# When the expert rows of three token groups are gathered in a one-layer decoder step: all of the first two ahead of the one-hot gates, those of the last tile from its first pair of heads

## The chip, the cores and the metric

The kernel runs on one core of a Trainium2 chip (trn2). The metric is device time in microseconds (us) of one execution, from the runtime's own count; lower is better. The engines are named as in the profile: PE (TensorE matmul, with PEld its weight load), DVE (VectorE), ACT (ScalarE), POOL (GpSimd), SP (SyncE, which only issues DMAs here).

## The reference, cut to what matters

One layer of a decoder serves 512 prompt tokens (four tiles of 128) and 32 sample tokens. After the token mixing every token goes through an expert retrieval: for each of 8 heads it scores 128 + 128 sub-keys, takes the 16 best of each half, the 16 best of their sums, and so has 128 experts per token, each a row of `expert_u` and a row of `expert_v` (16384 x 1024 each, f32).

```
s1, i1 = lax.top_k(s[:, :, 0], PEER_TOPK)
s2, i2 = lax.top_k(s[:, :, 1], PEER_TOPK)
...
idx = jnp.take_along_axis(cidx, sel, axis=-1).reshape(PEER_BLOCK, PEER_HEADS * PEER_TOPK)
gate = jax.nn.softmax(top, axis=-1).reshape(PEER_BLOCK, PEER_HEADS * PEER_TOPK)
pre = jnp.einsum('td,tkd->tk', hb, eu[idx]).astype(F32)
act = jax.nn.gelu(pre, approximate=False) * gate
return jnp.einsum('tk,tkd->td', act.astype(hb.dtype), ev[idx])
```

## The kernel before, in words

The retrieval is done in two ways.

**Gathered**, for prompt tiles 0 and 3 and for the samples (`experts`, lines 1067 to 1100). For each k, POOL issues an indirect DMA (line 1075) that brings one row of `expert_u` per partition, 128 rows of 4 KB, into one of six buffers (tile `gat`); DVE multiplies it with the normed input and sums it (a *dot*: `CUSTOM_DVE_ANT_0` and the read of its sum into `pre`). When all dots are done, ACT applies Gelu, and the rows of `expert_v` come the same way; DVE adds each, scaled, to an accumulator `x` (an *add*: `SCALAR_TENSOR_TENSOR`). A prompt tile has 128 dots and 128 adds, the samples (packed four heads' groups to the partitions) have 32 and 32, and after them four small sums (tile `h`, 32x1024) and a norm, `finish` (line 1101). A row is used two gathers after it was issued (`LAG`), and the buffers are `GAT` = 6. Each gather is one step of a Python generator; `side` is the list of generators, and `beside(n)` takes n steps from the first of them.

**Dense**, for tiles 1 and 2. `gates` (line 1423) makes a 128 x 128 matrix of gates per token out of one-hot matmuls: for 8 tokens a step, DVE compares (tiles `uH`, `uL`, and two of eight columns in `vH`), ACT scales six columns, PE multiplies, ACT copies the result away. Sixteen steps make tile 1's gates, sixteen tile 2's. The gates also carry, by `next(more)`, the late part of tile 3: output projection, norm and query projection (`late`, line 1553). Then a loop over 128 blocks of experts (line 1644) does all 16384 experts for the 256 tokens: per block PE transposes and multiplies, DVE makes the low parts `uL`, `aL` and applies the gates (`w`), ACT casts, POOL makes `vL` (line 1498).

**What sets the order.** All engines work their queues in order. The queues are written at compile time by a scheduler that takes instructions in the order of the code (of *tracing*) as long as its own timeline says they can start; `tc.issue_after(m)` adds that what is traced inside stands behind instruction `m` on its engine. Before, the rows of tile 0 and of the samples are 320 gathers: 280 steps (`AHEAD`) are traced by a loop ahead of the gates, each only bound to stand behind the DVE instruction that was last when tile 0's rows were put on the list; during the 32 gate steps 0.8 steps each (`RATE_G`), behind the last DVE instruction of that gate step; the rest in the dense loop, 1.6 steps a block (`RATE_H`) as long as tile 3 is being decoded and 2.4 (`RATE_D`) after that.

The decode of tile 3 (`late_heads`, line 1607) runs one step a block in the dense loop. Its 8 heads come as four pairs. Two pairs share the second half of `head_steps` (line 995): the first pair only finds its top 16, then the second pair does so and the index work is done for all four heads. After two pairs (64 of 128 columns of `ei` known) tile 3's rows are put on the list.

```
1619    for n in range(AHEAD):
1620        with tc.issue_after(marks[gather_mark[0]]):
1621            beside(1)
1622    more = late()
...
1652        next(more, None)
1653        with tc.issue_after(mark), tc.issue_after(sub):
1654            beside(RATE_H if coming[0] else RATE_D)
```

Of the kernel before, what the change touches and what calls it, by code (L numbers as in the profile page):

```python
# [32 lines left out]
LAG = 2  # L33
WST = 3
UV = 5
AHEAD = 280
RATE_G = 0.8
RATE_D = 2.4
RATE_H = 1.6
LATE = 2  # L40
# [69 lines left out]
def bc(ap, shape):  # L110
    return ap.to_broadcast(shape)
# [3 lines left out]
def hymba_step(ctx, tc, x_prompt, x_sample, cache_k, cache_v, state_wkv, state_shift, meta, norm1_g, w_in, mu, w0,  # L115
# [4 lines left out]
    marks = []  # L120
# [124 lines left out]
    side, due = [], [0.0]  # L245

    def beside(n):

        due[0] += n
        while side and due[0] >= 1.0:  # L250
            due[0] -= 1.0
            if next(side[0], None) is None:
                side.pop(0)
        due[0] = min(due[0], 1.0)
# [875 lines left out]
    def tile_experts(i, ei, ga, h2, x2=None):  # L1130
        def mk():
            if x2 is None:
                box.append(px2())
                G.dma_start(box[0], xscr[i])
            return box[0]
        box = [] if x2 is None else [x2]
        yield from experts(h2, ei, ga, 128, mk, False)
        finish(box[0], gat(), 128, y_p[0, 128 * i:128 * i + 128, :], final_g(gat()))
# [15 lines left out]
    def place(c):  # L1154
        return _t(p0, "ei" + c, 1, [128, 128], I32), _t(p0, "ga" + c, 1, [128, 128])

    plS, pl0, pl1 = place("s"), place("0"), place("1")
# [46 lines left out]
    with ExitStack() as px:  # L1204
# [43 lines left out]
        def put(src, dst):  # L1248

            A.copy(dst[0], src)  # L1250
            V.tensor_tensor(dst[1], src, dst[0].bitcast(F32), OP.subtract)
# [171 lines left out]
    def gates(its, sel, ps, put):  # L1423


        i1T, i2T, gaT = sel
        its, iot = its
        ib = dt_("aH", 2, [128, 2, 128], BF16)
        for c, x in enumerate((i1T, i2T)):
            A.copy(ib[:, c], x)  # L1430
        for n, t8 in enumerate(range(0, 128, 8)):
            ob = dt_("uL", 2, [128, 128, GA], BF16)
            o0, o1 = dt_("uH", 2, [128, 8, 128]), dt_("vH", 2, [128, 8, 128])
            V.tensor_tensor(o0.rearrange("p t j -> p j t"), its, bc(ib[:, 0, t8:t8 + 8].unsqueeze(1), [128, 128, 8]), OP.is_equal)
            V.tensor_tensor(ob, its[:, :, 0:GA], bc(ib[:, 1, t8:t8 + GA].unsqueeze(1), [128, 128, GA]), OP.is_equal)
            for q0 in (0, 4):
                p = ps()
                for q in range(q0, q0 + 4):
                    t = slice(t8 + q, t8 + q + 1)
                    if q < GA:  # L1440
                        A.mul(o1[:, q, :], ob[:, :, q], gaT[:, t])
                    else:
                        V.tensor_scalar(o1[:, q, :], iot, i2T[:, t], gaT[:, t], OP.is_equal, OP.mult)
                    T.matmul(p[:, 128 * (q - q0):128 * (q - q0) + 128], o0[:, q, :], o1[:, q, :], start=True, stop=True)  # L1444
                put(t8 + q0, p)
            if n % LATE:
                next(more, None)
            with tc.issue_after(marks[-1]):
                beside(RATE_G)


    ND = 256
# [3 lines left out]
    def dt_(tag, bufs, shape, dt=F32):  # L1456
        return _t(dn, tag, bufs, shape, dt)
# [148 lines left out]

    def late_heads():

        half = None
        for g in range(4):  # L1610
            if g == 2:
                side.append(tile_experts(3, *pl1, held[0]))
            sc = dt_("lsc", 1, [128, 4, 128])
            DM.dma_start(sc, lscr[g])
            half = yield from head_steps(sc, [x[:, 32 * (g & 2):32 * (g & 2) + 64] for x in pl1], late_tile, half if g % 2 else [])
            yield True
        coming[0] = False

    for n in range(AHEAD):
        with tc.issue_after(marks[gather_mark[0]]):  # L1620
            beside(1)
    more = late()
    its = one_hot_table()
    sels = [sel_transposed(0, dps, dt_("selT", 1, [128, 3, 128])), sel_transposed(1, dps, dt_("lsc", 1, [128, 3, 128]))]
    gates(its, sels[0], dps, stage)
    gates(its, sels[1], dps, keep)
    for _ in more:
        pass
    more = late_heads()
    gl = {}  # L1630

# [68 lines left out]
```

## Time and profile before

| | us |
|---|---|
| three runs | 2180.15, 2190.67, 2161.02; median 2180.15 |
| the profiled execution | 2171.7 |
| its span in the trace | 2169.9 |
| PE, DVE, ACT, POOL busy | 1816.4, 1639.2, 862.6, 1271.9 |

The span is first to last instruction; what lies around it is 1.8 us. The shares of busy time are means over stages that have different limits: the projection and mixing (0 to about 1085 us), the gates (about 1116 to 1247), the dense loop (about 1247 to 2131) and a tail. A line of the grouped views reads: line, engine, operation, written tile <- read tiles, shapes, count | busy time in us, mean ns of one | idle time of the engine just before them and what ended it. All DVE instructions have one line (127, a helper), so they go by tiles.

### The profile page before, as it was taken

To read this page: it belongs to the slowest core of one execution; us is meant where nothing else is said; L and a number is where in the kernel's file an instruction comes from. 1 tells how busy PE (TensorE), PEld (TensorE's weight loads), DVE (VectorE), ACT (ScalarE), POOL (GpSimd) and SP (SyncE) were. 2 spreads that over 40 slices of the span, in tenths; PEclk is the share of its full clock that TensorE was granted. 3 is DMA by queue.
4 is the path that set the end of the run, shared out by engine and by line. 5 is a ranking of instruction groups with operands and counts; after the bars stand their busy time and mean duration, and the time that the engine had idled before them with its cause. 6 is when DMAs were issued, how large, how long until landed. Compare 5 with 4: busy or idle time off the path is not lost.

```text
span 2169.9 us, 37101 instructions
## 1 busy us (share of the span) xinstructions
PE 1816.4 (84%) x13915; PEld 1693.1 (78%) x13915; DVE 1639.2 (76%) x3285; ACT 862.6 (40%) x1975; POOL 1271.9 (59%) x951
## 2 busy tenths in 40 slices
PE   5999984585685868898567998999999999999992
PEld 5888973373574757798457988899999999999992
DVE  5643426679878988678989999867676767899988
ACT  6553421221132322433258943444444444444442
POOL 0110103678777677533824365768776777888885
PEclk9999986555675768799769999999999999999996
DMA  7532373487779789966859985789999998999987
GB/s 222 164 107 81 106 199 108 156 304 237 262 247 308 242 282 323 299 222 206 271 182 330 341 287 191 287 297 392 336 336 336 330 338 330 326 322 328 328 312 261
DMA packets 311306, 571.60 MB, mean 263 GB/s; under 512 B 32916, under 2 KB 194694, under 8 KB 310983
## 3 DMA queue, kind: packets, MB, share of 16 engines
q0 software_dynamic: 84048, 305.70, 39.6%
q1 hardware_dynamic: 227078, 263.53, 37.5%
q8 instruction: 110, 1.80, 0.3%
q14 instruction: 70, 0.57, 0.1%
HBM read 544.12 MB, written 25.65 MB: 263 GB/s over the span
## 4 chain that ended last, share of the span: by engine, by line
PE 56%; DVE 17%; issue 9%; DMA 8%; POOL 7%; ACT 3%; SPq 0%; POOLq 0%; DVEq 0%; ACTq 0%
PE acc L1523 5%; PE acc L1524 5%; PE acc L1522 5%; PE w L1508 5%; PE w L1505 5%; PE w L1506 5%; PE w L1491 4%; POOL gat L1075 4%; PE pD L220 3%; DVE x L127 3%; PE pD L966 2%; DVE gat L127 2%; DMA wst<-in_w_query_dram 2%; PE ps L220 2%; PE w L1444 2%
## 5 line engine op out<-in xcount | busy, mean ns | idle before, releaser
L127 DVE SCALAR_TENSOR_TENSOR x<-gat,act,x 128x1024 f32<-128x1024 f32 x287 | 440.5, 1535 | 12.5 <-DMA gat<-in_expert_v_dram,ei 9.4
L1075 POOL DMA_INDIRECT gat<-in_expert_u_dram,ei x256 | 337.0, 1316 | 132.2 <-DVE pre L127 45.8
L1075 POOL DMA_INDIRECT gat<-in_expert_v_dram,ei x256 | 317.7, 1241 | 122.6 <-issue 35.4
L1498 POOL TENSOR_TENSOR vL<-uv,vH 128x1024 fp32r<-128x1024 f32 x128 | 335.2, 2619 | 84.0 <-ACT vH L1497 82.7
L1522 PE MATMUL acc<-aH,vH 128*128 128x256 f32 x1024 | 292.2, 294 | 6.2 <-ACT aH L1514 6.2
L1523 PE MATMUL acc<-aL,vH 128*128 128x256 f32 x1024 | 289.5, 285 | 7.0 <-DVE aL L127 6.8
L1524 PE MATMUL acc<-aH,vL 128*128 128x256 f32 x1024 | 288.6, 284 | 0.0
L1505 PE MATMUL w<-dhH,uH 128*128 128x256 f32 x1024 | 251.6, 283 | 2.7 <-DVE uL L127 1.5
L1506 PE MATMUL w<-dhL,uH 128*128 128x256 f32 x1024 | 251.3, 283 | 0.0
L127 DVE CUSTOM_DVE_ANT_0 gat<-gat,h 128x1024 f32<-128x1024 f32 x160 | 202.7, 1279 | 44.7 <-DMA gat<-in_expert_u_dram,ei 41.7
L1523 PEld LDWEIGHTS acc<-aL,vH 128*128 128x128 f32 x1024 | 197.2, 193 | 8.9 <-DVE aL L127 8.8
L1505 PEld LDWEIGHTS w<-dhH,uH 128*128 128x128 f32 x1024 | 196.7, 192 | 3.1 <-DVE uL L127 1.7
L1522 PEld LDWEIGHTS acc<-aH,vH 128*128 128x128 f32 x1024 | 192.7, 192 | 7.1 <-ACT aH L1514 7.1
L1524 PEld LDWEIGHTS acc<-aH,vL 128*128 128x128 f32 x1024 | 197.1, 192 | 0.0
L1506 PEld LDWEIGHTS w<-dhL,uH 128*128 128x128 f32 x1024 | 196.7, 192 | 0.0
L1497 ACT CAST vH<-uv 128x1024 fp32r<-128x1024 f32 x128 | 134.9, 1054 | 148.9 <-issue 111.3
L127 DVE TENSOR_TENSOR uL<-w,uH 128x512 fp32r<-128x512 f32 x256 | 166.7, 682 | 10.1 <-ACT uH L1493 10.1
L127 DVE TENSOR_TENSOR w<-w,gl 128x128 f32<-128x128 f32 x128 | 50.3, 393 | 148.6 <-ACT w L1509 148.6
L127 DVE CUSTOM_DVE_ANT_0 gat<-gat,lx 128x1024 f32<-128x1024 f32 x128 | 158.1, 1268 | 0.0
L1508 PE MATMUL w<-dhH,uL 128*128 128x256 f32 x1024 | 148.1, 286 | 4.7 <-DVE uL L127 4.3
L1493 ACT CAST uH<-w 128x512 fp32r<-128x512 f32 x256 | 138.0, 593 | 8.0
L1508 PEld LDWEIGHTS w<-dhH,uL 128*128 128x128 f32 x1024 | 133.0, 192 | 7.6 <-DVE uL L127 6.9
(568 smaller groups left out, 4046.5 us busy)
## 6 DMA issues: line engine op xcount, KB each, us to landing
uv<-in_expert_u_dram SPq DMA_DIRECT2D x128, 512.0 KB, 4.5
uv<-in_expert_v_dram SPq DMA_DIRECT2D x128, 512.0 KB, 6.0
wst<-in_w_query_dram SPq DMA_DIRECT2D x48, 512.0 KB, 6.6
wst<-in_w_out_dram SPq DMA_DIRECT2D x24, 512.0 KB
wst<-in_w_in_dram SPq DMA_DIRECT2D x20, 512.0 KB, 4.4
h2T<-in_w_in_dram SPq DMA_DIRECT2D x20, 512.0 KB, 4.2
gscr<-uv SPq DMA_DIRECT2D x10, 1024.0 KB, 5.9
uv<-in_w_query_dram SPq DMA_DIRECT2D x8, 1024.0 KB, 12.2
```

Of the source, the lines that this page charges most:

```text
L127: r = getattr(nc.vector, name)(*args, **kw)
L220: T.matmul(p[:, 0:n], w[:, k, :], x, start=(k == 0 and x is H and w is wH), stop=(k == 7 and w is wL))
L1075: G.indirect_dma_start(out=r, out_offset=None, in_=w[0], in_offset=bass.IndirectOffsetOnAxis(ap=ei[:, k:k + 1], axis=0))
L1493: A.copy(uH[:, ks, :], p)
L1497: A.copy(vH, vn)
L1498: G.tensor_tensor(vL, vn, vH.bitcast(F32), OP.subtract)
L1505: T.matmul(pre, uH[:, k, :], hH[:, k, :], start=(k == 0), stop=False)
L1506: T.matmul(pre, uH[:, k, :], hL[:, k, :], start=False, stop=False)
L1508: T.matmul(pre, uL[:, k, :], hH[:, k, :], start=False, stop=(k == 7))
L1522: T.matmul(o, vH[:, ds_], aH, start=(j == 0 and d % 2 == 0), stop=False, skip_group_check=True)
L1523: T.matmul(o, vH[:, ds_], aL, start=False, stop=False, skip_group_check=True)
L1524: T.matmul(o, vL[:, ds_], aH, start=False, stop=(j == 127), skip_group_check=True)
```

## The change

1. All steps of the rows of tile 0 and of the samples are traced ahead of the gates (`while side`), and `gates` takes none any more.
2. Tile 3 is decoded pair by pair: each pair runs the whole of `head_steps` by itself, for 2 heads, and its rows are put on the list after the first pair instead of the second.

```
-AHEAD = 280
-RATE_G = 0.8
...
             if n % LATE:
                 next(more, None)
-            with tc.issue_after(marks[-1]):
-                beside(RATE_G)
...
     def late_heads():
 
-        half = None
         for g in range(4):
-            if g == 2:
+            if g == 1:
                 side.append(tile_experts(3, *pl1, held[0]))
             sc = dt_("lsc", 1, [128, 4, 128])
             DM.dma_start(sc, lscr[g])
-            half = yield from head_steps(sc, [x[:, 32 * (g & 2):32 * (g & 2) + 64] for x in pl1], late_tile, half if g % 2 else [])
+            yield from head_steps(sc, [x[:, 32 * g:32 * g + 32] for x in pl1], late_tile)
             yield True
         coming[0] = False
 
-    for n in range(AHEAD):
+    while side:
         with tc.issue_after(marks[gather_mark[0]]):
             beside(1)
```

The rates in the dense loop (1.6 and 2.4) stay. PE's queue is the same up to the first transposes of the dense loop. Three places of the queues follow.

DVE just ahead of the gates: `dsel` is the decode of tile 2 that ends there, `dhL` a low part for the dense loop, `uH` and `vH` the first gate step. Before:

```order
L127 TENSOR_REDUCE dsel_16_111<-ce_7163 128x32
L127 TENSOR_TENSOR ce_7167<-iota_87,hl_7152 128x512
L127 TENSOR_REDUCE dsel_17_112<-ce_7167 128x32
L127 TENSOR_TENSOR ce_7171<-iota_87,hl_7152 128x512
L127 TENSOR_REDUCE dsel_17_112<-ce_7171 128x32
L127 TENSOR_TENSOR dhL<-w_7873,dhH 128x4x128
L127 TENSOR_TENSOR dhL<-w_7880,dhH 128x4x128
L127 TENSOR_TENSOR dhL<-w_7889,dhH 128x4x128
L127 TENSOR_TENSOR dhL<-w_7896,dhH 128x4x128
L127 TENSOR_SCALAR vH_8792<-aL_8771,selT_8775 128x128 x2
L127 TENSOR_TENSOR uH_8791<-vL_8773,aH_8787 128x128x8
```

The same place now; `x_1953` is the samples' accumulator:

```order
L125 TENSOR_REDUCE dsel_17_112<-ce_7171 128x32
L125 SCALAR_TENSOR_TENSOR x_1953_8803<-gat_8847,act_8800,x_1953_8803 128x1024
L125 SCALAR_TENSOR_TENSOR x_1953_8803<-gat_8850,act_8800,x_1953_8803 128x1024
L125 SCALAR_TENSOR_TENSOR x_1953_8803<-gat_8853,act_8800,x_1953_8803 128x1024
L125 SCALAR_TENSOR_TENSOR x_1953_8803<-gat_8856,act_8800,x_1953_8803 128x1024
L125 TENSOR_TENSOR dhL<-w_7873,dhH 128x4x128
L125 SCALAR_TENSOR_TENSOR x_1953_8803<-gat_8859,act_8800,x_1953_8803 128x1024
L125 TENSOR_TENSOR dhL<-w_7880,dhH 128x4x128
L125 SCALAR_TENSOR_TENSOR x_1953_8803<-gat_8862,act_8800,x_1953_8803 128x1024
L125 TENSOR_TENSOR dhL<-w_7889,dhH 128x4x128
L125 TENSOR_TENSOR dhL<-w_7896,dhH 128x4x128
L125 TENSOR_SCALAR vH_8950<-aL_8929,selT_8933 128x128
```

Counted over the whole queue, 11 dots and 22 adds have moved to a place ahead of the first `uH`. The sixteen steps of tile 1's gates had 11 dots and 1 add between them and now have 10 adds, the four small sums and the samples' last scaling; those of tile 2's gates had 12 adds and now none.

DVE in the dense loop's second and third block: `lvals`, `lidx`, `lsc` and `lcand` belong to the decode of tile 3, `x_2051` is the samples' accumulator. Before:

```order
L127 TENSOR_TENSOR uL_10286<-w_10287,uH_10285 128x512
L127 TENSOR_TENSOR uL_10286<-w_10294,uH_10285 128x512
L127 SCALAR_TENSOR_TENSOR x_2051_9243<-gat_10244,act_9240,x_2051_9243 128x1024
L127 MAX lvals_10608<-lsc_10606 128x8 x2
L127 TENSOR_TENSOR aL_10279<-w_10250,aH_10278 128x256
L127 MAX lvals_10608<-lsc_10606 128x8 x2
L127 MAX_INDEX lidx_10230<-lvals_10608,lsc_10606 128x8 x4
L127 MATCH_REPLACE lsc_10606<-lvals_10608,lsc_10606 128x128 x4
L127 MAX lvals_10608<-lsc_10606 128x8 x4
```

Now; `lsm` and `leq` are the index work that before came only after the second pair, `ei` the finished row numbers:

```order
L125 TENSOR_TENSOR uL_10264<-w_10265,uH_10263 128x512
L125 TENSOR_TENSOR uL_10264<-w_10272,uH_10263 128x512
L125 TENSOR_TENSOR aL_10257<-w_10228,aH_10256 128x256
L125 TENSOR_REDUCE lsm_10683<-leq_10767 128x32
L125 MAX lvals_10944<-lsc_10939 128x8 x4
L125 SCALAR_TENSOR_TENSOR ei_11_106<-lsm_10682,lsm_10683 128x32
L125 MAX_INDEX lidx_10941<-lvals_10944,lsc_10939 128x8 x4
L125 MATCH_REPLACE lsc_10939<-lvals_10944,lsc_10939 128x128 x4
L125 MAX lvals_10944<-lsc_10939 128x8 x3
```

Between the last gate step and the 18th `aL`, 19 adds, the four small sums and the scaling are gone, 15 dots of tile 3 stand there instead of 5, and the decode has some 25 instructions more. The row numbers were finished after `aL` 9 and 17 (two pairs each) and are finished after `aL` 2, 5, 9 and 12.

DVE at the end: `uv` is the dense tiles' output, `x_3149` and `x_3145` tile 3's accumulator. Before, with three more adds, a reciprocal and the last scaling behind these rows:

```order
L127 SCALAR_TENSOR_TENSOR uv_21365<-uv_21365,sE_21381,uv_21335 128x1024
L127 SCALAR_TENSOR_TENSOR x_3149_16489<-gat_20635,act_16486,x_3149_16489 128x1024
L127 SCALAR_TENSOR_TENSOR x_3149_16489<-gat_20638,act_16486,x_3149_16489 128x1024
L127 SCALAR_TENSOR_TENSOR x_3149_16489<-gat_20722,act_16486,x_3149_16489 128x1024
L127 SCALAR_TENSOR_TENSOR x_3149_16489<-gat_20725,act_16486,x_3149_16489 128x1024
L127 SCALAR_TENSOR_TENSOR x_3149_16489<-gat_20728,act_16486,x_3149_16489 128x1024
L127 SCALAR_TENSOR_TENSOR x_3149_16489<-gat_20810,act_16486,x_3149_16489 128x1024
L127 SCALAR_TENSOR_TENSOR x_3149_16489<-gat_20813,act_16486,x_3149_16489 128x1024
L127 SCALAR_TENSOR_TENSOR x_3149_16489<-gat_20895,act_16486,x_3149_16489 128x1024
L127 SCALAR_TENSOR_TENSOR x_3149_16489<-gat_20898,act_16486,x_3149_16489 128x1024
L127 SCALAR_TENSOR_TENSOR x_3149_16489<-gat_20901,act_16486,x_3149_16489 128x1024
L127 SCALAR_TENSOR_TENSOR x_3149_16489<-gat_20983,act_16486,x_3149_16489 128x1024
```

Now, to the end of the work:

```order
L125 SCALAR_TENSOR_TENSOR uv_21427<-uv_21427,sE_21443,uv_21397 128x1024
L125 SCALAR_TENSOR_TENSOR x_3145_16314<-gat_20721,act_16311,x_3145_16314 128x1024
L125 SCALAR_TENSOR_TENSOR x_3145_16314<-gat_20724,act_16311,x_3145_16314 128x1024
L125 SCALAR_TENSOR_TENSOR x_3145_16314<-gat_20808,act_16311,x_3145_16314 128x1024
L125 SCALAR_TENSOR_TENSOR x_3145_16314<-gat_20811,act_16311,x_3145_16314 128x1024
L125 SCALAR_TENSOR_TENSOR x_3145_16314<-gat_20814,act_16311,x_3145_16314 128x1024
L125 SCALAR_TENSOR_TENSOR x_3145_16314<-gat_20896,act_16311,x_3145_16314 128x1024
L125 RECIPROCAL sF_20906<-sF_20906 128x1
L125 SCALAR_TENSOR_TENSOR gat_20901<-x_3145_16314,sF_20906,gat_20902 128x1024
```

Behind the last `aL` there were 22 adds and are 14. On POOL, behind the last `vL`, there were 21 gathers and are 12.

## Rows read from the trace of the kernel before

**Rows 1.** Busy time by stage; times are us from the span's start.
```profile
core 0: us, PE busy (x) PEld busy (x) DVE busy (x) ACT busy (x) POOL busy (x), PEclk, DMA share, GB/s
1021.00:1085.00 64.00, 35.04 (x254) 31.85 (x252) 60.29 (x184) 15.73 (x46) 54.33 (x52) 0.83 0.87 276
1085.00:1115.70 30.70, 15.82 (x62) 11.92 (x62) 25.40 (x121) 9.71 (x26) 9.69 (x15) 0.50 0.66 211
1115.70:1172.00 56.30, 39.61 (x256) 36.51 (x256) 53.29 (x83) 47.07 (x121) 20.63 (x10) 0.89 0.79 261
1172.00:1247.00 75.00, 74.32 (x616) 72.05 (x617) 67.29 (x88) 69.80 (x241) 28.18 (x16) 0.97 0.96 332
1247.00:1397.00 150.00, 132.77 (x1048) 127.68 (x1048) 141.96 (x365) 64.88 (x124) 93.38 (x74) 0.97 0.71 249
1397.00:2125.00 728.00, 723.84 (x6104) 722.54 (x6103) 568.44 (x897) 303.64 (x544) 567.39 (x340) 1.00 0.91 330
2125.00:2161.40 36.40, 5.96 (x38) 5.43 (x37) 33.26 (x32) 8.64 (x22) 21.91 (x19) 0.59 0.90 328
```
**Rows 2.** The chain that ended last, from 2100 us on: start, us, what.
```profile
2103.60 0.96 PE w L1508 x8
...
2110.22 0.48 PE w L1508 x4
...
2153.61 6.36 DMA gat<-in_expert_v_dram,ei
2160.06 1.29 DVE x L127
```
**Rows 3.** Issues of SP's queue in order of time, 2080 to 2171.
```profile
2138.64 2.73 SPq L1103 DMA_DIRECT2D out_dram<-uv  x2
2165.61 0.33 SPq L1103 DMA_DIRECT2D out_dram<-gat  x1
```
**Rows 4.** DVE groups, 1085 to 1115.7: line, op, shapes, count | busy, mean ns | idle before.
```profile
L127 DVE TENSOR_REDUCE dsel<-ce 128x32 f32<-128x512 f32 x5 | 3.4, 684 | 4.6 <-POOL ce L1053 4.6
```
**Rows 5.** DVE groups, 1021 to 1087.
```profile
L127 DVE CUSTOM_DVE_ANT_0 gat<-gat,h 128x1024 f32<-128x1024 f32 x21 | 31.7, 1515 | 2.7 <-DMA gat<-in_expert_u_dram,eis 2.7
```
**Rows 6.** DVE groups, 780 to 950.
```profile
L127 DVE SCALAR_TENSOR_TENSOR x<-gat,act,x 128x1024 f32<-128x1024 f32 x71 | 97.1, 1367 | 5.9 <-DMA gat<-in_expert_v_dram,ei 5.4
```
**Rows 7.** DVE groups, 1115.7 to 1172.
```profile
L127 DVE TENSOR_TENSOR uH<-vL,aH 128x1024 f32<-128x1024 bf16 x14 | 26.9, 1934 | 0.0
L127 DVE CUSTOM_DVE_ANT_0 gat<-gat,h 128x1024 f32<-128x1024 f32 x10 | 12.1, 1214 | 0.0
...
L127 DVE DVE_READ_ACCUMULATOR2_ANT pre<- 128x1 f32 x10 | 0.8, 78 | 0.0
```
**Rows 8.** DVE groups, 1172 to 1247.
```profile
L127 DVE SCALAR_TENSOR_TENSOR x<-gat,act,x 128x1024 f32<-128x1024 f32 x13 | 16.7, 1281 | 0.0
```
**Rows 9.** DVE groups, 1247 to 1397.
```profile
L127 DVE SCALAR_TENSOR_TENSOR x<-gat,act,x 128x1024 f32<-128x1024 f32 x18 | 35.3, 1964 | 0.0
...
L127 DVE CUSTOM_DVE_ANT_0 gat<-gat,lx 128x1024 f32<-128x1024 f32 x6 | 10.6, 1786 | 0.0
...
L127 DVE TENSOR_TENSOR h<-h,gat 32x1024 f32<-32x1024 f32 x3 | 4.8, 1584 | 0.4 <-DMA gat<-x 0.4
...
L127 DVE SCALAR_TENSOR_TENSOR gat<-h,sF,gat 32x1024 f32<-32x1024 f32 x1 | 1.3, 1262 | 0.0
...
L127 DVE TENSOR_TENSOR ga<-ga,sR 128x64 f32<-128x64 f32 x2 | 0.4, 211 | 0.0
```
**Rows 10.** DVE groups, 2125 to 2161.4.
```profile
L127 DVE SCALAR_TENSOR_TENSOR x<-gat,act,x 128x1024 f32<-128x1024 f32 x23 | 29.5, 1283 | 2.5 <-DMA gat<-in_expert_v_dram,ei 2.1
```
**Rows 11.** POOL groups, 1021 to 1087.
```profile
L1075 POOL DMA_INDIRECT gat<-in_expert_u_dram,eis x26 | 33.4, 1284 | 10.9 <-issue 3.4 <-DVE pre L127 1.9 <-DVE hl L127 1.8
```
**Rows 12.** POOL groups, 1115.7 to 1247.
```profile
L1075 POOL DMA_INDIRECT gat<-in_expert_v_dram,eis x20 | 38.0, 1900 | 61.0 <-DVE x L127 44.9 <-DVE pre L127 15.8 <-DVE uL L127 0.3
```
**Rows 13.** POOL groups, 1247 to 1397.
```profile
L1498 POOL TENSOR_TENSOR vL<-uv,vH 128x1024 fp32r<-128x1024 f32 x19 | 46.8, 2464 | 18.2 <-ACT vH L1497 18.1
```

More of the change, by code (lines that the diff above doesn't have):

```diff
@@ L35 @@
 UV = 5
-AHEAD = 280
-RATE_G = 0.8
 RATE_D = 2.4
@@ L1447, in gates @@
                 next(more, None)
-            with tc.issue_after(marks[-1]):
-                beside(RATE_G)
     ND = 256
@@ L1607, in late_heads @@
     def late_heads():
-        half = None
         for g in range(4):
-            if g == 2:
+            if g == 1:
                 side.append(tile_experts(3, *pl1, held[0]))
@@ L1614, in late_heads @@
             DM.dma_start(sc, lscr[g])
-            half = yield from head_steps(sc, [x[:, 32 * (g & 2):32 * (g & 2) + 64] for x in pl1], late_tile, half if g % 2 else [])
+            yield from head_steps(sc, [x[:, 32 * g:32 * g + 32] for x in pl1], late_tile)
             yield True
         coming[0] = False
-    for n in range(AHEAD):
+    while side:
         with tc.issue_after(marks[gather_mark[0]]):
```

## The prediction

> **What bounds the kernel now.** I read the table by stage first, because the shares over the whole span mix stages with different limits [rows 1]. The reader should go down its rows and ask which engine fills each stretch. From 1085 to 1115.7 (stage A, end of the decode ahead of the gates) it is DVE: 25.4 of 30.7 us, and the 5.3 us that it idles are mostly waits for POOL's `ce`, 4.6 us in front of one group [rows 4]. From 1115.7 to 1172 (B1, gates of tile 1) it is DVE again, 53.3 of 56.3. From 1172 to 1247 (B2, gates of tile 2 with the query projection) it is PE: 74.3 of 75.0; DVE has 7.7 us to spare. From 1247 to 1397 (C, first blocks of the dense loop) DVE is busy for 142 of 150 and PE for 132.8; so PE waits 17.2 us there. From 1397 to 2125 (D) PE has 723.8 of 728: the chain steps from one L1508 to the next in 2110.22 - 2103.60 = 6.62 us [rows 2], and 728 us are 110 blocks of 6.62. After 2125 PE is done but for a little, and the chain goes through the last gathers and adds of tile 3 [rows 2] while DVE has 33.3 of 36.4 us and the DMA engines 0.90 at 328 GB/s [rows 1]. The dense tiles' output is on its way long before the last one: SP issues it from 2138.64 and tile 3's at 2165.61 [rows 3].
>
> So a DVE instruction in A, B1 or the tail costs its duration; in B2 and D it is free as long as DVE keeps its slack; in C it is worth something until PE's 17.2 us are used up.
>
> **The change, part by part.** The queue listings say what moves; the trace says for what price.
>
> *A: 11 dots and 22 adds come in.* A dot took 1.515 us just before this place, beside the same work [rows 5], with 0.078 for the read of its sum [rows 7]. An add took 1.367 in an earlier stretch where POOL also mainly gathered [rows 6]. That is 11 x 1.593 + 22 x 1.367 = 47.6 us. DVE's own 5.3 us of idle can take some of it; I count 4, as the work is interleaved with the decode that waits for `ce`: +43. From below: the gates' prices, 1.214 + 0.078 and 1.281 [rows 7, 8], and all idle filled, 42.4 - 5.3 = +37. From above: C's prices, 1.786 + 0.078 and 1.964 [rows 9], and no idle filled, +64. Rows 5 and 6 are the nearest, so I stay near the lower end. Can POOL supply the rows? About 33 gathers (9 of `expert_u`, 24 of `expert_v`) at 1.284 [rows 11] and some 0.3 between them are 52 us, with 8 us of POOL's other work here (9.7 less two gathers) 60, in a stretch that becomes 74 us long. It fits, without much to spare.
>
> What is queued behind the moved adds is the first `uH`, and for it wait PE's and ACT's gates. Nothing in front of the gates hides the 43 us.
>
> *B1.* Out go 11 dots and 1 add, 11 x 1.292 + 1.28 = 15.5; in come 10 adds, four sums `h` and the scaling, 10 x 1.281 + 4 x 1.584 + 1.26 = 20.4 [rows 7 to 9]. DVE had 3.0 us of gaps. +4, from 0 (gaps taken, ACT limits) to +9 (DVE also waits for the small DMA that brings `gat` for `h`).
>
> *B2.* 12 adds go out, 12 x 1.281 = 15.4 us of DVE. PE fills the stretch, so they lay beside PE's work and what is saved is nothing: 0, at most -3. This is where the change gives away cover: the same adds are paid in A.
>
> *C.* 18 adds, the sums and the scaling leave: 35.3 + 6.3 + 1.3 = 42.9 us [rows 9]. Ten dots come earlier, 10 x 1.864 = 18.6, and some 25 short decode instructions at about 0.2, the price of the `ga` row [rows 9], add 5. DVE's work falls from 142 to about 123, below PE's 132.8, so PE's 17.2 us of waiting is what can be had. Part of it stays: the four pairs of heads are now decoded within 12 blocks, in runs of short DVE instructions in front of `uL` and `aL`. I take -12, range -17 to -4. The adds that leave are the dearest of the kernel, 1.964 against 1.281.
>
> *D.* 10 dots leave and 8 adds enter, beside a PE that is busy for 99.4%: 0, from -2 to +3.
>
> *Tail.* 8 adds fewer at 1.283 [rows 10] are 10.3 us. By the other limit, 9 gathers fewer of 0.524 MB (128 rows of 4 KB) at 328 GB/s [rows 1] are 9 x 1.60 = 14.4 us. I take -12, range -15 to -8. What is late next is the dense output: its second write is issued at 2141.4, and with the 4.3 us that the last one takes from its issue to the end of the span (2169.9 - 2165.61) it would end near 2145.7, so up to 24 us could go before it decides.
>
> *Sum:* 43 + 4 + 0 - 12 + 0 - 12 = +23 us on the profiled execution, 2171.7 + 23 = 2194.7. That execution lies 8.5 us under the median of the runs shown; the mean of all four executions is 2175.9. I put the sum on that mean: 2199.
>
> **A rule against the rows.** An add takes 1.964 us in C, where POOL runs a `vL` of 2.464 us per block [rows 9, 13], and 1.281 us in B2, where POOL only gathers [rows 8, 12]. The Trainium skill (SBUF — State Buffer, section "Who interferes with whom") says that a DVE instruction with two SBUF inputs contends with a GpSimd instruction that reads SBUF, and that the one that comes second is blocked until the first has finished. By that rule, the rows agree: 0.68 us more per add beside `vL`. By the rule the adds moved into A, beside few POOL reads, would cost the 1.28 of the gates and not 1.37 or more; A would then be +37 and the sum +17.
>
> **The rivals.**
>
> 1. *The moved rows cost the low price.* If adds in A run as in the gates, A is +37 and the sum +17: 2193. For it: rows 8 are the same instruction beside the same gathers. Against it: rows 5 and 6, nearer in place and with the same decode around, are dearer.
>
> 2. *All is given back.* A at +37, B1 +2, C all of its 17 us, and the tail as far as the dense output, -24: together -2, 2174. For it: the tail's adds wait for DMA, so that fewer of them could be lighter than in proportion. Against it: 14 adds and two norms' scalings still stand behind the last block, 14 x 1.283 = 18 us of DVE alone, and C must lose every wait.
>
> 3. *Rows come too slowly in A* (the other side). DVE works in order; each add waits there for its row, a row for one of six buffers, and a buffer for an earlier add. In 1021 to 1087, 26 gathers took 66 us, 2.54 us each [rows 11]; in B1 and B2 one took 1.900 us of POOL alone [rows 12]. If 33 rows go at 3.1 us each, A is 102 us long, +72, and the sum is +52: 2228. It decides over the forecast from 74 / 33 = 2.2 us per row on. For it: 2.54 is already over that point. Against it: in that stretch POOL waited for DVE or for work only 10.9 us and had two long `ax` and other work between, and in the tail the rows come at 1.6 us.
>
> That the change does not do what it says is excluded by the queues: no step of the first two groups stands in B2 any more.
>
> **How the numbers follow.** The forecast 0.58, rival 1 0.20, rival 2 0.12, rival 3 0.10. The forecast's own range, with C between -17 and -4, the tail between -15 and -8 and A between 39 and 55, is about 2183 to 2216. The range for 8 in 10 reaches from rival 2 to rival 3, 2172 to 2228; single runs of before differ by 30 us already. A measurement of this kernel can tell about 2% from no change, 44 us: 2136.5 and 2223.8. Only rival 3 passes the upper one: slower 0.09; no case passes the lower: faster 0.01; within 0.90.
>
> **What would show it.** In the profile after: the first `uH` about 43 us later than 1115.7; B1 some 4 us longer; B2 still 75 us with PE full; the PE idle time between the end of the gates and the 18th block under 10 us instead of 17.2; D in steps of 6.62; and between the last `aL` and the last add about 24 us instead of 36. I am wrong if the gates begin less than 30 us later (then DVE had room in A that the table does not show), if B2 shrinks without its adds (then DVE, not PE, set it), or if DVE's idle time in A grows by more than 10 us and names gathers (rival 3).

## The result and the profile after

Each kernel was run 20 times. Before: 2168.19 us in the median (2159.2 to 2190.67). After: 2192.86 us (2181.71 to 2204.67). The ratio is 1.0109, with a 95% interval of 1.0091 to 1.0127: about 24 us slower. The forecast was 2199, +23 on its own base.

The profiled execution of after took 2185.24 us, with a span of 2183.5, so the two profiles lie only 13.6 us apart, against 24.7 between the medians. The rest is in code that the change does not touch: the row numbers of the samples (`eis`) are written at 1020.7 us before and at 1008.4 after. All stages are therefore measured from that write on, which is 1149.1 us before and 1175.0 after, +25.9.

Stages after, with the columns of [rows 1]; the cuts are the write of `eis`, the first `uH`, the 17th, the last, the 18th `aL`, the last `aL`, the end of the span:

```profile
core 0: us, PE busy (x) PEld busy (x) DVE busy (x) ACT busy (x) POOL busy (x), PEclk, DMA share, GB/s
1008.40:1141.20 132.80, 50.89 (x318) 44.51 (x317) 125.34 (x351) 29.63 (x77) 108.97 (x99) 0.66 0.90 306
1141.20:1218.80 77.60, 56.49 (x346) 53.08 (x347) 65.75 (x87) 56.66 (x145) 12.66 (x10) 0.79 0.74 221
1218.80:1276.70 57.90, 57.75 (x495) 56.09 (x494) 42.32 (x59) 54.83 (x199) 0.00 (x0) 1.00 0.75 246
1276.70:1418.90 142.20, 130.15 (x1035) 126.57 (x1036) 115.20 (x386) 70.86 (x141) 82.58 (x70) 0.96 0.66 233
1418.90:2150.20 731.30, 727.82 (x6149) 727.34 (x6148) 597.52 (x891) 305.99 (x549) 580.09 (x338) 1.00 0.91 328
2150.20:2183.50 33.30, 5.95 (x38) 5.42 (x37) 24.44 (x26) 11.34 (x29) 13.12 (x12) 0.60 0.71 253
```

The same cuts in the kernel before (its dense loop is in [rows 1]):

```profile
1020.70:1115.70 95.00, 51.16 (x318) 44.07 (x317) 85.99 (x306) 25.49 (x72) 64.02 (x66) 0.72 0.80 255
1115.70:1183.90 68.20, 51.37 (x346) 48.26 (x347) 61.09 (x95) 56.82 (x143) 24.45 (x13) 0.89 0.81 269
1183.90:1241.80 57.90, 57.76 (x495) 56.12 (x495) 55.91 (x71) 54.85 (x199) 23.42 (x12) 1.00 0.97 332
1241.80:1394.20 152.40, 135.21 (x1060) 129.48 (x1059) 142.78 (x365) 69.61 (x143) 91.54 (x74) 0.97 0.73 256
...
2125.00:2169.90 44.90, 5.96 (x38) 5.43 (x37) 34.71 (x34) 11.33 (x29) 21.91 (x19) 0.58 0.76 278
```

Read row against row (the last two columns are the busy share of the DMA engines and what they moved). Up to the first `uH`: 95.0 to 132.8, DVE 86.0 to 125.3 busy, so DVE's idle time stays (9.0 and 7.5) and the added work is nearly all paid. Tile 1's gates: 68.2 to 77.6, with only 4.7 us more DVE work. Tile 2's gates: 57.9 both times, PE full, though DVE now works 42.3 instead of 55.9 and POOL nothing. The end of the gates with the first 18 blocks: 152.4 to 142.2, DVE from 142.8 to 115.2. The dense loop: 730.8 to 731.3. Behind the last `aL`: 44.9 to 33.3.

DVE groups of after between the write of `eis` and the first `uH` (they answer to [rows 4 to 6]):

```profile
L125 DVE CUSTOM_DVE_ANT_0 gat<-gat,h 128x1024 f32<-128x1024 f32 x32 | 43.4, 1362 | 3.2 <-DMA gat<-in_expert_u_dram,eis 3.2
L125 DVE SCALAR_TENSOR_TENSOR x<-gat,act,x 128x1024 f32<-128x1024 f32 x21 | 28.5, 1357 | 1.0 <-DMA gat<-in_expert_v_dram,eis 0.9
...
L125 DVE TENSOR_REDUCE dsel<-ce 128x32 f32<-128x512 f32 x8 | 5.4, 679 | 3.3 <-POOL ce L1051 3.3
...
L125 DVE DVE_READ_ACCUMULATOR2_ANT pre<- 128x1 f32 x32 | 2.5, 78 | 0.0
```

Eleven more dots than the 21 of [rows 5] cost 43.4 - 31.7 = 11.7 us, 1.06 each; the adds cost 1.357. The dense loop still goes in steps of 6.62 (2135.69 - 2129.07), and the end still hangs on the last gathers and adds, as in [rows 2]:

```profile
2129.07 0.96 PE w L1504 x8
...
2135.69 0.96 PE w L1504 x8
...
2165.34 8.48 DMA gat<-in_expert_v_dram,ei
2173.91 1.30 DVE x L125
```

and the adds behind the last `aL`, 15 where [rows 10] has 23, cost the same:

```profile
L125 DVE SCALAR_TENSOR_TENSOR x<-gat,act,x 128x1024 f32<-128x1024 f32 x15 | 19.2, 1281 | 1.4 <-DMA gat<-in_expert_v_dram,ei 1.2
```

### The profile page after: what moved, and what is told of

Its sections match the earlier page's. It is cut to its first block, busy times and chain, and to the rows that moved or that the text cites. A ratio compares the mean times of both kernels' runs of the same rounds, so it can differ in the third digit from the quotient of the medians.

```text
span 2183.5 us, 37145 instructions
## 1 busy us (share of the span) xinstructions
PE 1806.7 (83%) x13915; PEld 1690.0 (77%) x13915; DVE 1659.9 (76%) x3311; ACT 869.3 (40%) x1985; POOL 1274.2 (58%) x955
## 4 chain that ended last, share of the span: by engine, by line
PE 58%; DVE 15%; DMA 9%; issue 8%; POOL 6%; ACT 4%; SPq 0%; POOLq 0%; DVEq 0%; ACTq 0%
PE acc L1520 5%; PE acc L1519 5%; PE acc L1518 5%; PE w L1504 5%; PE w L1501 5%; PE w L1502 5%; PE w L1487 5%; POOL gat L1073 4%; PE pD L218 3%; DVE gat L125 3%; PE pD L964 2%; DVE x L125 2%; DMA wst<-in_w_query_dram 2%; PE ps L218 2%; DMA m<-mscr 2%
## 5 line engine op out<-in xcount | busy, mean ns | idle before, releaser
L125 DVE SCALAR_TENSOR_TENSOR x<-gat,act,x 128x1024 f32<-128x1024 f32 x287 | 449.0, 1564 | 11.6 <-DMA gat<-in_expert_v_dram,ei 7.6
L1073 POOL DMA_INDIRECT gat<-in_expert_v_dram,ei x256 | 328.9, 1285 | 120.1 <-issue 38.9
L125 DVE CUSTOM_DVE_ANT_0 gat<-gat,lx 128x1024 f32<-128x1024 f32 x128 | 168.9, 1354 | 0.0
L1504 PE MATMUL w<-dhH,uL 128*128 128x256 f32 x1024 | 146.2, 285 | 0.4 <-DVE uL L125 0.4
```

Of the source, the lines that this page charges most:

```text
L125: r = getattr(nc.vector, name)(*args, **kw)
L1073: G.indirect_dma_start(out=r, out_offset=None, in_=w[0], in_offset=bass.IndirectOffsetOnAxis(ap=ei[:, k:k + 1], axis=0))
L1504: T.matmul(pre, uL[:, k, :], hH[:, k, :], start=False, stop=(k == 7))
```

## The experiments

All were timed beside the kernel before, in three groups (runs 1 to 4, 5 to 8, 9 to 11); the groups have before at 2167.5, 2171.1 and 2172.6 us, so runs of different groups are compared by their ratios. The table is worked out from the starts of the cut instructions in each run's trace (us); "sum" is all from the write of `eis`, as a difference to before. Each row is one execution. Runs 8 and 11 are the same kernel: their stages lie up to 1.0 us apart and their sums 3.1, and differences of that size are not read.

| run | to first `uH` | gates 1 | gates 2 | to 18th `aL` | dense | tail | sum | ratio of times (95%) |
|---|---|---|---|---|---|---|---|---|
| before | 95.0 | 68.2 | 57.9 | 152.3 | 730.8 | 44.9 | | |
| after | 132.8 | 77.6 | 57.9 | 142.1 | 731.3 | 33.3 | +25.9 | 1.0109 (1.0091 to 1.0127) |
| 1 rows ahead alone | 131.5 | 77.9 | 57.9 | 134.0 | 733.5 | 45.3 | +30.9 | 1.0138 (1.011 to 1.0165) |
| 2 pairs alone | 95.2 | 67.8 | 57.9 | 159.2 | 734.8 | 43.2 | +9.0 | 1.0036 (1.0014 to 1.0059) |
| 3 18 beside gates 2 | 118.2 | 65.9 | 60.2 | 146.4 | 731.1 | 34.0 | +6.6 | 1.0041 (1.0011 to 1.0071) |
| 4 two decode steps | 130.8 | 77.5 | 57.9 | 152.5 | 730.7 | 18.8 | +19.1 | 1.0105 (1.0073 to 1.0137) |
| 5 3, and 12 beside gates 1 | 105.8 | 69.0 | 60.5 | 146.2 | 728.9 | 33.7 | -5.0 | 0.9984 (0.9959 to 1.0009) |
| 6 5, two steps | 106.6 | 68.2 | 60.2 | 157.9 | 730.2 | 19.0 | -6.9 | 1.0002 (0.9978 to 1.0025) |
| 7 16 and 24, two steps | 95.5 | 73.3 | 63.6 | 161.0 | 734.8 | 20.5 | -0.5 | 1.0021 (0.9997 to 1.0044) |
| 8 14 and 20, two steps | 94.6 | 72.2 | 62.5 | 151.6 | 734.3 | 22.9 | -11.1 | 0.9949 (0.992 to 0.9978) |
| 9 8 with one step | 94.3 | 72.1 | 62.5 | 152.5 | 733.2 | 33.1 | -1.6 | 1.0012 (0.998 to 1.0044) |
| 10 before, 14 and 20 | 94.1 | 71.5 | 62.5 | 134.3 | 732.5 | 45.4 | -8.7 | 0.9955 (0.9924 to 0.9987) |
| 11 8 again | 94.0 | 72.5 | 62.5 | 150.7 | 733.3 | 22.0 | -14.2 | 0.9968 (0.9942 to 0.9995) |

**1. Part one alone.** The changed kernel with the decode of before:

```
-            if g == 1:
+            if g == 2:
...
-            yield from head_steps(sc, [x[:, 32 * g:32 * g + 32] for x in pl1], late_tile)
+            half = yield from head_steps(sc, [x[:, 32 * (g & 2):32 * (g & 2) + 64] for x in pl1], late_tile, half if g % 2 else [])
```

> All 320 steps ahead of the gates as in the changed kernel, but tile 3 decoded as before (two pairs share the index work, its rows on the list after the second pair). Theory 'cover' (the loss is the rows that left places where they lay beside PE): A +38, B1 +9, gates to dense +1, block 1 to 18 between -12 and -17 (19 adds, the sums and the scaling leave, no dots come), tail 0 (22 adds still stand behind the last block): +31 to +36, 2199 to 2204. Rival 'decode' (the shorter first blocks come from the early pairs, and the pairs' own short instructions are part of the loss): the first 18 blocks stay within 4 us of before, +44 or more, 2212 and up. Rival 'tail' (the tail is shorter because the rows of the samples are out of the way, not by the early list): the tail loses 8 us or more here too, +23 or less.

Measured: 2198.27 against 2167.52 us.

```profile
1018.20:1149.80 131.60, 51.00 (x318) 44.29 (x317) 124.56 (x352) 29.61 (x77) 110.14 (x99) 0.66 0.90 307
1149.80:1227.60 77.80, 57.12 (x346) 53.61 (x347) 65.67 (x87) 56.66 (x145) 12.61 (x10) 0.79 0.73 223
...
1285.50:1419.50 134.00, 127.39 (x1035) 124.99 (x1035) 101.27 (x338) 66.18 (x132) 67.91 (x56) 0.97 0.60 215
...
2153.00:2198.30 45.30, 5.82 (x39) 5.45 (x38) 34.59 (x34) 11.34 (x29) 22.08 (x19) 0.58 0.76 274
```

All of the loss ahead of the dense loop is here, and none of the tail's gain. The first blocks fall to 134.0, 18.3 under before: the rows that left bring that alone, and the early pairs of the change cost 8.1 us of it (142.1 - 134.0), for a tail that is 12.0 shorter. That is "cover", with a little more from the first blocks than its 12 to 17; "decode" and "tail" fall.

**2. Part two alone.** The kernel before with `late_heads` of the change.

> Tile 3 decoded pair by pair and listed after the first pair, but 280 steps ahead and 0.8 a gate step as before. Theory 'cover': A, B1 and B2 as before; the list still holds steps of the samples for the first nine blocks, so the early list brings only 3 dots more into the first 18 blocks and takes 2 adds out of the tail; DVE is the bound of the first blocks, so 3 dots and some 25 short instructions cost +5 to +10 there, the tail gives -2.6: +2 to +8, 2170 to 2176. Rival 'decode': the pairs alone cost +15 or more. Rival 'tail by the list': the tail gives its 12 us here too, -4 or less.

Measured: 2175.88 against 2167.52.

```profile
1236.50:1395.80 159.30, 134.82 (x1035) 129.03 (x1036) 148.26 (x395) 75.45 (x151) 97.61 (x82) 0.96 0.74 259
```

DVE has 148.3 of the 159.3 us of the first blocks, which got 6.9 longer, as expected; the tail gave 1.7. The dense loop is 4.0 longer, which was not expected and stays open. So neither part shortens the tail alone (45.3 in run 1, 43.2 here, 33.3 together): the two need each other there. That this is so because the samples' steps must be out of the list before tile 3's rows are on it is read from the order of the list; run 9, which has six steps left there, fits (33.1).

**3. Rows beside tile 2's gates.** The changed kernel with

```
+AHEAD = 302
+RATE_G = (0.0, 1.125)
...
-    while side:
+    for n in range(AHEAD):
...
-    gates(its, sels[0], dps, stage)
-    gates(its, sels[1], dps, keep)
+    gates(its, sels[0], dps, stage, RATE_G[0])
+    gates(its, sels[1], dps, keep, RATE_G[1])
```

and `beside(rate)` behind `marks[-1]` in each gate step, as before.

> The changed kernel, with 302 steps ahead of the gates, none beside tile 1's gates and 18 beside tile 2's. Counted on DVE against the changed kernel: 11 adds fewer ahead of the gates, 10 adds and the sums fewer in tile 1's gates, 18 adds in tile 2's gates where there were none, 3 adds, the sums and the scaling in the first blocks. Theory 'cover': A -14, B1 -10 to -17, B2 +5 (DVE 42.3 + 23 is over PE's 57.8), first blocks +2 to +6: -12 to -24 against the changed kernel, 2169 to 2181. Rival 'no cover' (an add beside the PE of tile 2's gates costs its duration): B2 +15 to +23, so within 8 us of the changed kernel, 2185 and up.

Measured: 2177.11, 15.8 us under after (ratios 1.0041 and 1.0109).

```profile
1025.80:1144.00 118.20, 52.34 (x323) 45.67 (x322) 109.37 (x340) 28.76 (x75) 97.89 (x89) 0.69 0.89 299
1144.00:1209.90 65.90, 51.81 (x347) 49.02 (x348) 48.76 (x72) 55.15 (x141) 0.00 (x0) 0.84 0.66 200
1209.90:1270.10 60.20, 59.04 (x506) 57.28 (x505) 60.20 (x76) 57.04 (x208) 36.13 (x15) 1.00 0.98 341
```

Sixteen of the eighteen adds begin between the cuts, and tile 2's gates get 2.3 us longer: 0.14 us each for an instruction of 1.3. That is a mean over two kinds. Before, twelve adds there cost nothing (57.9 with and without them); here DVE is busy for all of the 60.2 us (55.9 of 57.9 before), and the last four cost 0.6 each. Taken from the place ahead of the gates, eleven adds give 14.6 back. The DMA engines are busy for 0.98 of the stage, against 0.75 after and 0.97 before; no run shows that they limit it.

**4. Two steps of decode per block.** The changed kernel with

```
-        next(more, None)
+        for _ in range(2):
+            next(more, None)
         with tc.issue_after(mark), tc.issue_after(sub):
```

> The changed kernel, with two steps of tile 3's decode per block instead of one, so that its rows are listed some four blocks earlier: 10 dots more in the first 18 blocks (from block 5 instead of 9), no add behind the last block instead of 14. Theory 'cover': DVE has 22 us to spare in the first 18 blocks of the changed kernel, PE waits 7.8 us there: +0 to +8; the tail loses 13 of its 33 us before the dense output decides: -5 to -14 against the changed kernel, 2179 to 2188. Rival 'bandwidth' (the tail's rows only move to where the DMA engines are as full, 0.91 in the dense loop): the dense loop grows by the 10 to 13 us that the tail loses, 2190 or more.

Measured: 2189.72, 3.1 us under after; by its ratio, 1.0105 against 1.0109, it is not apart from it, by its trace it is 6.8 us shorter.

```profile
1277.80:1430.30 152.50, 135.31 (x1041) 131.30 (x1041) 135.28 (x402) 70.99 (x141) 93.20 (x77) 0.93 0.69 242
1430.30:2161.00 730.70, 726.70 (x6144) 726.20 (x6142) 570.19 (x890) 306.91 (x548) 562.66 (x341) 1.00 0.91 333
2161.00:2179.70 18.70, 6.00 (x37) 5.54 (x36) 7.11 (x12) 10.32 (x29) 0.00 (x0) 0.69 0.21 85
```

The dense loop did not grow (730.7), so "bandwidth" falls, but the dots that come earlier cost 10.4 us in the first blocks where I expected 8 at most. Eight of them begin between the cuts, not ten. DVE's idle time there (142.2 - 115.2 = 27.0 us after; I had counted 22) was not free: the 23 dots took 1.597 us on average, where the 15 of after had taken 1.284.

```profile
L125 DVE CUSTOM_DVE_ANT_0 gat<-gat,lx 128x1024 f32<-128x1024 f32 x23 | 36.0, 1597 | 0.0
```

and after:

```profile
L125 DVE CUSTOM_DVE_ANT_0 gat<-gat,lx 128x1024 f32<-128x1024 f32 x15 | 18.8, 1284 | 0.0
```

The tail went from 33.3 to 18.8, and its chain now goes through the dense output, as the prediction's rival 2 had it for a tail 24 us shorter:

```profile
2161.04 0.35 DVE aL L125
...
2167.36 1.28 DVE gat L125
...
2169.27 1.16 ACT uv L195 x2
...
2174.17 1.63 DVEq L1692
```

Behind the last `aL` and PE's products come the dense tiles' `uv`, and no add.

**5. Rows beside both gates.** Run 3 with `AHEAD = 290` and `RATE_G = (0.75, 1.125)`.

> The run with 18 rows beside tile 2's gates, with 290 steps ahead and 12 beside tile 1's gates: counted on DVE, 11 adds stand in tile 1's gates instead of ahead of the gates, and nothing else moves. Theory 'shared bound' (tile 1's gates are set by DVE and ACT in turn; without rows that stage took 65.9 us, with 12 rows 68.2 before): tile 1's gates +2 to +5, A -13: -8 to -11 against that run, 2166 to 2169. Rival 'DVE bound' (the prediction's: an instruction in tile 1's gates costs its duration): +14 and -13, within 3 us of that run, 2174 to 2180.

Measured: 2169.52, ratio 0.9984, no difference to before that can be measured.

```profile
1023.80:1129.50 105.70, 52.06 (x323) 44.95 (x321) 95.62 (x329) 28.61 (x75) 80.98 (x78) 0.69 0.86 280
1129.50:1198.60 69.10, 52.99 (x352) 50.33 (x353) 60.90 (x83) 55.96 (x143) 19.74 (x11) 0.85 0.82 258
```

The eleven adds cost 12.4 us less ahead of the gates and 3.1 more in tile 1's gates, where DVE has 12.1 us more to do than in run 3. "Shared bound" holds in its price, 0.3 us an add; that DVE and ACT limit the stage in turn is its explanation and was not shown. Against run 3 the run is 11.5 us shorter by its trace and some 12 by the ratios (0.9984 and 1.0041).

**6. Run 5 with two steps.**

> The run before it in this list, with two steps of tile 3's decode per block: 10 dots more in the first 18 blocks, 2 adds behind the last block instead of 14. Theory 'neutral trade' (seen where the changed kernel got two steps: first blocks +10.4, tail -14.5): -3 to -5 against that run. Theory 'dearer here' (the first blocks also hold the samples' sums and three adds, so each dot there costs its 1.8 us): first blocks +15 to +19, so 0 to +5.

Measured: 2172.99, ratio 1.0002. First blocks +11.7, tail -14.7: between the two expectations, and by its time not apart from run 5. Inconclusive.

**7. More beside the gates.** 280 ahead, `RATE_G = (1.0, 1.5)`, two steps.

> 280 steps ahead, 16 beside tile 1's gates, 24 beside tile 2's, two steps of decode per block. Counted on DVE: nothing more ahead of the gates than before the change but one dot, 10 dots and 5 adds in tile 1's gates, 24 adds in tile 2's, 3 adds and the sums in the first blocks. Theory 'shared bound': A 0, tile 1's gates +2 to +6; in tile 2's DVE has 42 + 31 = 73 us against PE's 57.8, so +10 to +15; first blocks +0 to +5, tail -24: -2 to -12 against before, 2156 to 2165. Rival 'bandwidth' (24 rows of 0.524 MB in 58 us are over what the DMA engines move): tile 2's gates +20 or more, 2172 and up.

Measured: 2176.4, ratio 1.0021: over the first expectation, and in the range of the second without its reason. Tile 2's gates took only 5.7 us more, half of the least I expected, so the rows are not too many for it; but tile 1's gates took 5.1 more, the first blocks, with tile 3's dots from the seventh on, 8.7 (161.0), and the dense loop 4.0, and all of these together ate the tail's 24.4.

**8. Fewer beside the gates.** 280 ahead, `RATE_G = (0.9, 1.25)`, two steps.

> 280 steps ahead, 14 beside tile 1's gates, 20 beside tile 2's, two steps of decode per block. Counted on DVE: nothing more ahead of the gates than before, 11 dots and 3 adds in tile 1's gates, 20 adds in tile 2's, 9 adds, the sums and 22 dots in the first blocks, 6 adds behind the last block. Theory 'shared bound': A 0, tile 1's gates +2 to +3, tile 2's +4 to +6, first blocks +6 to +10 (9 adds fewer, 15 dots more than before), tail -18 to -20: 0 to -6 against before, 2162 to 2168. Rival 'dearer first blocks': +15 or more there, 2170 and up.

Measured: 2159.0 against 2171.13, ratio 0.9949, faster than both kernels and by more than the 0 to 6 us expected: the first blocks did not grow at all (151.6 against 152.3) and the tail gave 22.0.

**9. Run 8 with one step.**

> The run with 14 rows beside tile 1's gates and 20 beside tile 2's, but one step of tile 3's decode per block, as in the changed kernel. Counted on DVE against that run: 6 dots fewer in the first 18 blocks, 14 adds behind the last block instead of 6. Theory 'neutral trade': first blocks -6 to -8, tail +10: +2 to +5 against that run, 2162 to 2166. Rival 'early list pays': first blocks the same, +8 to +11, 2168 to 2171.

Measured: 2173.77. The first blocks stay (152.5 against 151.6) and the tail is 33.1: the rival was right, the early list pays here. Why five dots fewer between the cuts gave nothing stays open.

**10. Before, with run 8's gates.** `RATE_G = (0.9, 1.25)` and nothing else; the decode is that of before.

> The kernel before, with 14 rows beside tile 1's gates and 20 beside tile 2's instead of 13 and 13, and tile 3 decoded as before. Counted on DVE: 2 adds more in tile 1's gates, 7 more in tile 2's, 9 fewer in the first blocks, 22 adds behind the last block as before. Theory 'cover': tile 1's gates +4, tile 2's +4.6 (72.2 and 62.5 us in the run with the same gates, 68.2 and 57.9 before), the first blocks lose 9 adds at 1.0 to 1.96, -9 to -18: -1 to -9, 2162 to 2170. Rival 'first blocks are not set by their adds': they give under 5, +4 or more, 2175 and up.

Measured: 2159.18 against 2172.56, ratio 0.9955, faster than both kernels.

```profile
1111.00:1182.50 71.50, 53.09 (x353) 49.43 (x354) 63.06 (x97) 57.57 (x144) 26.88 (x15) 0.85 0.80 266
1182.50:1245.00 62.50, 58.48 (x499) 56.55 (x499) 62.50 (x78) 57.67 (x210) 39.66 (x18) 1.00 1.00 358
1245.00:1379.30 134.30, 128.17 (x1050) 125.96 (x1049) 122.41 (x351) 67.86 (x132) 82.77 (x66) 0.99 0.73 261
```

Eight adds went from the first blocks to the gates by the starts in the trace (I had counted nine). The blocks took 18.0 us less, as much as where all 19 adds, the sums and the scaling had left them (run 1, 134.0): PE is now busy for 128.2 of 134.3 us, and the eleven adds that are left cost nothing. The gates took 3.3 + 4.6 more, for two adds and for six: behind the first eleven or twelve the places in the gates are dear. Runs 8, 10 and 11 are not apart by their ratios, so beside these gates the early decode shows no gain of its own.

**11. Run 8 again.**

> The run with 14 rows beside tile 1's gates and 20 beside tile 2's and two steps of decode per block, the same kernel once more. If its gain is the kernel's, 0.992 to 0.998 of before again, and the part behind the query of the samples' rows 1138 us, 11 under before, whatever the part ahead of it takes; if it was the part ahead, which was short there, the ratio goes to 1.

Measured: 2163.77 against 2172.56, ratio 0.9968.

The gain is the kernel's: 14.2 us behind the write of `eis`, though that write came 9.6 us later (1022.6) than in run 8 (1013.0).

## Why the prediction was right, step by step

**A, the part that had to come first: right in kind, 5 us too large.** Forecast +43, measured +37.8 from the write of `eis` on. The dots were mis-sized: 11 x 1.593 = 17.5 stood in the sum, and they took 11.7 + 0.9 for their reads = 12.6. The 1.515 of [rows 5] is a mean over two kinds. Going through the trace of before one dot at a time, 12 dots that overlapped a computing instruction of POOL (not a gather) took 1.742 on average and 9 that did not took 1.213; after, 16 and 16 took 1.513 and 1.211. Dots over 1.3 us were seven before and five after: the added ones came at the low price. The idle time was also wrong, the other way: of 4 us counted as filled, 1.5 were. Together with 1.7 us less of other work: 12.6 + 28.5 (21 of the 22 adds are in the rows; the samples' first is another instruction) - 1.7 - 1.5 = 37.9.

The adds' mean came out (1.367 forecast, 1.357 measured), but by luck. One of the 21 took 2.986 us and the 20 others 1.275 on average; in run 4, which has the same adds in this place, none was long:

```profile
L125 DVE SCALAR_TENSOR_TENSOR x<-gat,act,x 128x1024 f32<-128x1024 f32 x21 | 26.8, 1275 | 0.9 <-DMA gat<-in_expert_v_dram,eis 0.7
```

So rival 1 had the size (+37) and for the adds also the reason, the low price of the gates; its filled idle time (all 5.3 us) did not come. The rule of the Trainium skill (SBUF — State Buffer, section "Who interferes with whom") agrees with the dense loop of after, where 44 adds that began behind a computing POOL instruction took 2.790 on average and 35 of 36 that began ahead of one took the price of a clear add (last section). In A only five adds overlapped a computing POOL instruction: four took 1.25 to 1.28 like the 16 others (1.277, none over 1.285), and one is the long one, which began 0.6 us ahead of POOL's `ce`, so that the order of the rule does not explain it. I had the rule, with few POOL reads in A, and still took the dearer row.

The prediction called itself wrong if the gates began less than 30 us later. Against the span's start they began 1141.2 - 1115.7 = 25.5 later; but 12.3 us of that comparison lie ahead of all moved rows, in the same code. The mark should have been set from the write of `eis`; as it was written, the sign came, and measured from that write on (37.8) it did not.

**B1: the size was wrong, and its reason.** Forecast +4, measured +9.4. DVE's work grew by 65.75 - 61.09 = 4.7, as counted. What failed is "a DVE instruction in B1 costs its duration", in both directions: run 5 put eleven adds there for 3.1 us, run 10 two more than before for 3.3. The prediction's cut at 1172 also ends two steps short of tile 1's sixteen ([rows 7] have 14 `uH`); they end at 1183.9. What the change brings in besides adds is the end of the samples (four sums, a norm, a scaling) beside tile 3's norm. Run 5 without that end has 69.0, after has 77.6. But run 5 also has less DVE work (60.9 us). Run 7, without that end and with 64.9 us of DVE work there, takes 73.3. As an estimate from these two, about 5 of the 9.4 us come with work of any kind, and about 4 are left for the end of the samples. PE groups of before and of after in tile 1's gates:

```profile
L1444 PE MATMUL w<-vH,uH 128*128 128x128 f32 x240 | 33.0, 296 | 10.2 <-ACT vH L1441 10.1
```

```profile
L1442 PE MATMUL w<-vH,uH 128*128 128x128 f32 x240 | 36.4, 318 | 15.8 <-ACT vH L1439 9.4 <-DVE lx L125 3.8 <-DVE uH L125 2.6
...
L182 PE MATMUL w<-ident,lx 128*128 128x128 f32 x8 | 2.0, 428 | 8.4 <-DVE lx L125 8.4
```

The same products take longer, 318 ns instead of 296, and PE waits 8.4 us for `lx`, tile 3's normed rows, at L182. In the table by stretches PE's idle time is followed by the lower of the clock's two levels (columns as in [rows 1]):

```profile
1181.20:1191.20 10.00, 7.00 (x49) 6.31 (x48) 10.00 (x13) 7.66 (x19) 0.00 (x0) 0.98 0.80 261
1191.20:1201.20 10.00, 5.46 (x25) 4.97 (x24) 7.09 (x14) 9.97 (x28) 0.54 (x1) 0.67 0.53 157
1201.20:1211.20 10.00, 4.80 (x23) 4.80 (x24) 3.03 (x3) 4.59 (x14) 0.00 (x0) 0.50 0.75 224
1211.20:1221.20 10.00, 10.00 (x89) 9.89 (x89) 8.09 (x12) 9.02 (x25) 0.00 (x0) 0.99 0.47 130
```

PE is busy for 4.80 us of the ten from 1201.2 at a granted clock of 0.50 (its lower level, 1.2 of 2.4 GHz), and full at 0.99 ten us later. Behind the stage's first ten us, before has one row with a lowered clock (0.66 from 1165.7); after has these two and one of 0.71 from 1161.2. Over the stage the clock was 0.79, before it was 0.89, and PE's busy time went from 51.37 to 56.49 us for the same 346 instructions. How much of the 9.4 us is the clock's and how much the waits' was not tried apart.

**B2: right.** 0 forecast, 0.0 measured, and PE full. The twelve adds that left had been free; run 3 (16 adds, +2.3 us), run 10 (18, +4.6) and run 7 (19, +5.7) show where that ends.

**C: the size was right, the reason in half.** -12 forecast, -10.2 measured. Run 1 takes the sum apart: the rows that leave give 18.3, and the early decode takes 8.1 back. But this is not all PE's waiting. Between the cuts PE idled for 17.2 us before, 12.1 after (not under 10, as forecast) and 6.6 in run 1. The other 5.1 us are PE's work: 130.2 instead of 135.2 us, 1035 matmuls instead of 1060, as 25 begin only behind the 18th `aL`.

**D: right.** 0 forecast, +0.5 measured, steps of 6.62.

**Tail: right.** -12 forecast, -11.6 measured, and 1.28 us an add before and after.

**The sum:** forecast +23, +25.9 in the traces, +24.7 by the medians; A's 5 too much and B1's 5 too little cancel, which is luck. The rest of the distance from 2199 to 2192.9 is the base, 2175.9 from four executions, where 20 runs give 2168.2. The forecast's own range does not follow from the bounds named beside it: with A 39 to 55, C -17 to -4, the tail -15 to -8 and B1 at 4 the sum is +11 to +47, 2187 to 2223, not 2183 to 2216.

Of the rivals, "all is given back" had A right (+37), and fell by B1 (+9.4 where it has +2), C (-10.2 where it has -17) and the tail (-11.6 where it has -24), and "rows come too slowly" fell by DVE's idle time, 7.5 us of 132.8, with 3.2 and 0.9 us of it in front of groups that waited for rows.

## What to carry to other kernels

An instruction is worth what its stage gets shorter, not what it takes, and that changes with how many are there already. An add of 1.3 us cost 1.1 to 1.3 ahead of the gates (runs 5 and 3). Beside tile 1's gates eleven cost 0.3 each, and two more than before's twelve rows 1.6 each (runs 5 and 10). Beside tile 2's twelve were free, the next four cost 0.6 each and two more 1.1 each (before, runs 3 and 10), with DVE busy all the time in both runs. In the first dense blocks eight of the 19 cost 2.2 each, and the other eleven nothing (run 10 against before and run 1). So price a move from both of its ends, at the number that is there, and before a free place is emptied, see whether it can hold more: with the decode of before, moving eight adds into the gates (run 10) beat moving 33 instructions ahead of them (run 1) by 40 us of stage time, 39 by the medians. Compare stages from a cut behind which the code differs, not from the start of the span.

## What was not expected of the hardware

The same instructions up to the write of `eis` took from 1008.4 to 1036.9 us in the 13 profiled executions, more than the change is worth. In the stretch from 500 to 750 us, PE had 909 instructions at a granted clock of 0.66 in the execution with 1008.4, and 827 at 0.60 in the one with 1036.9. What comes first, the slower progress or the clock, was not tried.

An add or a dot takes the same in every stretch that was gone through as long as no computing POOL instruction overlaps it: 1.21 to 1.22 us on average for a dot and 1.28 for an add. Where one does, it counts which began first. In after's dense loop 34 dots that began ahead of the POOL instruction took 1.218 and nine that began behind it 3.034; of the adds, 36 that began ahead took 1.354, all but one of them the price of a clear one and that one 4.07, and 44 that began behind took 2.790. Before shows the same (dots 1.218 and 2.032, adds 1.342 and 2.878).
